# Moving eight heads' transposes from the matrix engine to the DMA crossbar, with the attention slots of a fused decoder layer planned anew

## The chip, the core and the metric

The kernel runs on one core of one Trainium2 chip. The metric is the device time of one execution in microseconds, the median of three runs; lower is better. The engines in the profile are PE (TensorE, matmuls, with PEld for its weight loads), DVE (VectorE), ACT (ScalarE), POOL (GpSimd) and SP (SyncE, which here issues DMAs only).

## What is computed

One layer of a hybrid decoder over 512 tokens of width 2048, all in float32. The normalised input is projected once and split into three attention branches; each branch's output is multiplied by SiLU of a gate path and projected back; the three are mixed by sigmoid gates, projected once more and added to the input. Cut to what matters here:

```python
proj = rms_norm(x, norm_gain) @ w_in
(qa, ka, va, za, qb, kb, vb, zb, fb, qc, zc, gate_logits) = split(proj)
# A: 12 query heads of 64, 4 key heads, sliding window of 128, blocks of 128, sinks, ALiBi
ya = sliding_window_attention(qa, ka, va, q_gain_a, k_gain_a, sinks_a)
#   p = exp(scores - m);  out = einsum('bnkgqs,bnskd->bnqkgd', p / denom, vb)
ua = (ya * silu(za)) @ w_branch_a
# B: 12 heads of 64, causal over all 512 keys, with the cumsum of log forget gates
yb = forgetting_attention(qb, kb, vb, fb + b_forget, q_gain_b, k_gain_b)
ub = (yb * silu(zb)) @ w_branch_b
# C: 4 heads of 128 into 256 memory tokens
yc = memory_attention(qc, *split(rms_norm(mem, mem_norm_gain) @ w_mem_kv), q_gain_c, k_gain_c)
uc = (yc * silu(zc)) @ w_branch_c
y = g[0] * ua + g[1] * ub + g[2] * uc          # g = sigmoid(gate_logits)
return x + y @ w_out
```

## The kernel before

**The stream.** The projections are a list of weight units. A unit is 256 rows of the weight matrix by up to 512 columns; SP loads it (`wa`), ACT rounds it to the matmul type (`wb`, two instructions, L212), DVE subtracts to get the low part (`wc`, two instructions, L215), and PE multiplies with high and low parts of the activations: high by high, low by high, high by low, 24 matmuls a unit (12 in the memory units). In the projections' order stand qB, kB, vB (branch B, two groups of six heads each: qB0, kB0, vB0, qB1, ...), qA0, qA1, kvA, z0, mem, qC, z1, z2 and z3. An unnormalised projection gathers in four PSUM banks, and an evacuation reads each bank when its last matmul is done (for V of branch B `evac` in L455 to L470, one ACT and one DVE instruction a bank).

**Slots.** Every third matmul of a unit calls `tick`, which moves the clock of slots by 0.5. Each attention head is a `Chain` of steps with an offset from the head's base slot; a step is written into the program when its slot has come and the resources that it takes (`free`: PSUM banks "T", the probability buffer "P", transposed buffers "PT", "S1", "S2", "RW" and more) are there. `later(dt, f)` writes an instruction so many slots further on. The tables at the top of the file (`BASES_*`, `STEPS_*`, `PREP_*`, `NORMS`, `EXP_*`, `DIV_*`, `LOW_*`, `PV_*`, `SUMS_X`) hold all these numbers:

```python
def tick():
    clock[0] += 0.5
    while agenda and agenda[0][0] <= clock[0]:
        heapq.heappop(agenda)[2]()
    for c in list(chains):
        c.advance()
```

PE, DVE, ACT and POOL run their instructions in the order in which they are written so. Nothing overtakes on an engine: what waits holds up all behind it.

**A head.** The keys and queries are normalised and transposed on PE (`tk`, `tq`); ACT copies the high parts and DVE subtracts the low ones (`qB`/`qA` by L547/L548, `kB`/`kA` by L558/L561, and `kl`, one of two buffers, by L559). PE makes the scores (`sB`, `sA`), twice each, with the key's high part and with `kl` (L585, L586). DVE adds the bias and takes the maximum, ACT takes the exponential with its row sums, and `scaled` (L590) divides by the sums: on DVE for branches B and C, on POOL for branch A. The probabilities `p` then have to be transposed for the product with V:

- Branch A, before: PE transposes the seven 128x128 blocks of a head (L721, L724, four and three of them, each group in a PSUM bank `ptA`), ACT casts each bank to `phA` (L565) and DVE subtracts `plA` (L567).
- Branch B, already before: POOL copies the float32 words into two planes of 16-bit halves (`s1B`), one transposing DMA turns them (`s2B`), ACT joins the halves (`ptB`, two copies, L648), ACT casts to `phB` (L656), DVE subtracts `plB` (L659).

Then PE multiplies with V (`avB`, `avA`, eight matmuls a head), ACT copies one half of the bank (`avs`) and DVE adds the other half (`ys`). When z0 is done, DVE scales its four banks (`zB`) and multiplies them into `ysB`; the sigmoid of SiLU stands on ACT much later, behind a load of its table (first at 538.7 us). `mhl` and `mraw` are the parts of the memory tokens.

After z3 the gates, the branch projections and the output projection follow, by a plan of their own.

Of the kernel before, what the change touches and what calls it, by code (L numbers as in the profile page):

```python
# [12 lines left out]
F32 = mybir.dt.float32  # L13
F32R = mybir.dt.float32r
# [22 lines left out]
BASES_C = (12.0, 19.5, 28.0, 33.5)
STEPS_B = (-11.5, -5.0, -2.5, -1.5, 0, 1, 2.0, 0.0, 3.0, 1.5, 10.0, 15.0, 17.5, 19.0, 24, 4.5)
STEPS_A = (-5.0, -1.0, -0.5, -1.5, 6.5, 8, 11, -6.5)
STEPS_C = (-8, -3.5, 0.5, 1, 8.0, 4.5, 10)  # L40

PREP_Q = ((0.0, 15.5, 41.0), (-1.5, 27.5, 50.5))
PREP_K = ((-0.5, 28.0, 40.5), (2.0, 30.5, 43.5))
PREP_A = (6, 18.5, 39.0, 46, 66.0, 76.5)
PREP_KA = (6.0, 32.5, 47.5, 68.0)

NORMS = {'qB0': (26.0, 4.5, 0.5), 'kB0': (10.5, 5.0, 3.5), 'qB1': (5.0, 3.5, 6.0), 'kB1': (6.5, 11.5, 3.5), 'qA0': (7.5, 4.0, 4.5), 'qA1': (10.0, 2.0, 1.5), 'kA': (2.5, 3, 0), 'mk': (1.0, 11.5, 6.5), 'qC0': (-1.0, 3, 0.5), 'qC1': (4.5, 7.0, 0.5)}
# [8 lines left out]
def tile_hybrid_block(ctx, tc, xT, x, memT, mem, ng, mng, w_in, b_forget, gqa, gka, sinks, gqb, gkb, gqc, gkc,  # L58
# [10 lines left out]
    def f32(ap):  # L69
        return ap.bitcast(F32)  # L70
# [521 lines left out]
    def head_B(h, kv):  # L592
# [92 lines left out]
    def head_A(h, kv):  # L685
        s = {}

        def sb():
            bi = s["bi"] = at.p.tile([P, S], F32, tag="bias", bufs=2, name=f"biA{h}")
            po.tensor_scalar(bi[:, :256], relt, -float(slopes[h]), None, op0=ALU.mult)  # L690

        def s1(pr):
            q, kh, kl, v, hv = kv()
            if pr == 0:
                p = at.p.tile([P, 1280], F32, tag="P", bufs=2, name=f"pA{h}")
                s["den"] = cp.tile([P, 16], F32, tag="den", bufs=2, name=f"denA{h}")
# [4 lines left out]
            for i in (2 * pr, 2 * pr + 1):
                c = P if i == 0 else 0
                scores(sb[:, i % 2, c:], q, kh, kl, i, slice(i * P - P + c, i * P + P))
            for i in (2 * pr, 2 * pr + 1):
                c = P if i == 0 else 0
                nm = den[:, 8 + i:9 + i]
                ve.tensor_tensor_reduce(out=pv[:, i, c:256], in0=sb[:, i % 2, c:], in1=bi[:, c:256], scale=-1.0,
                                        scalar=nsink[:, h:h + 1], op0=ALU.add, op1=ALU.min, accum_out=nm)
                later(EXP_A, lambda i=i, c=c, nm=nm: ac.activation(
                    pv[:, i, c:257], pv[:, i, c:257], AF.Exp, bias=nm, scale=-1.0, accum_out=den[:, i:i + 1]))  # L710
                later(DIV_A, lambda i=i, c=c: scaled(pv[:, i, c:256], den, i))

        def s2(g):
            pv = s["p"]
            if g == 0:
                s["hi"] = at.p.tile([P, 1280], F32R, tag="PH", bufs=1, name=f"phA{h}")
                s["lo"] = at.p.tile([P, 1280], F32R, tag="PL", bufs=1, name=f"plA{h}")
            tb = tbank(f"ptA{h}_{g}")
            c = 0
            for j in (2 * g, 2 * g + 1):  # L720
                pe.transpose(tb[:, c:c + P], pv[:, j, 128:256], ident)  # L721
# [923 lines left out]
```

## Time and profile before

| | us |
|---|---|
| median of three runs | 1470.73 (1470.09 to 1471.54) |
| the profiled execution | 1471.16 |
| its span | 1469.3 |
| PE busy | 1460.2 |
| DVE busy | 1095.3 |
| ACT busy | 759.0 |
| POOL busy | 245.6 |

The span runs from the first to the last instruction that the profiler shows; the 1.9 us between it and the execution's time lie around it. In the span, branch B's heads stand at some 110 to 355 us, branch A's at some 375 to 535, branch C's at some 540 to 615. In the rows that follow, the program's names stand without their numbers (`sB` is any head's score bank); a time in brackets is the idle time of the engine ahead of an instruction, and behind the arrow stands what ended it.

### The profile page before, as it was taken

The numbers are of one execution on the slowest core, as the hardware profiler recorded it, in microseconds if no ns is written. First come the engines' busy times: TensorE is split into PE (matmuls) and PEld (weight loads), VectorE is DVE, ScalarE is ACT, GpSimd is POOL, SyncE is SP. The second block draws the span as 40 slices with busy tenths as digits, with TensorE's granted clock in tenths as the row PEclk, the third lists the DMA queues.
The fourth block names the chain that finished last, engine by engine and source line by source line (L and its number), as shares of the span: only waits on it lengthen the run. The fifth ranks groups of instructions, "written<-read, shape, count | busy, mean of one in ns | idle before, by whom it ended". The sixth has DMA issues, their size and how long they took to land.

```text
span 1469.3 us, 20218 instructions
## 1 busy us (share of the span) xinstructions
PE 1460.2 (99%) x7073; PEld 1261.3 (86%) x7073; DVE 1095.3 (75%) x1862; ACT 759.0 (52%) x1212; POOL 245.6 (17%) x307
## 2 busy tenths in 40 slices
PE   9999999999999999999999999999999999999998
PEld 9999999988888888888888888888888888888887
DVE  6486776776687675479788788888887565689997
ACT  5546865874577564455344444444355354345442
POOL 0224762653333420000000000000000210110000
PEclk9999999999999999999999999999999999999999
DMA  8765565455355232676676676767676887666784
GB/s 294 222 205 159 132 155 161 120 143 157 108 163 158 72 101 72 206 256 221 199 236 205 221 226 214 228 209 249 208 231 214 271 237 199 222 244 220 243 293 147
DMA packets 166733, 287.35 MB, mean 196 GB/s; under 512 B 53596, under 2 KB 93148, under 8 KB 166632
## 3 DMA queue, kind: packets, MB, share of 16 engines
q1 hardware_dynamic: 161592, 269.54, 59.3%
q10 hardware_dynamic: 5040, 16.53, 3.4%
q8 instruction: 55, 0.90, 0.3%
q14 instruction: 46, 0.38, 0.1%
HBM read 244.58 MB, written 31.48 MB: 188 GB/s over the span
## 4 chain that ended last, share of the span: by engine, by line
PE 97%; ACT 2%; POOL 1%; DVE 0%; issue 0%; DMA 0%; SPq 0%; DVEq 0%; POOLq 0%; ACTq 0%
PE P L1118 41%; PE z L301 12%; PE qB L301 5%; PE vB L301 5%; PE uB L1118 4%; PE uA L1118 4%; PE kB L301 4%; PE mem L301 3%; PE qC L301 3%; PE kvA L301 3%; PE uC L1118 3%; PE qA L301 3%; PE avB L668 1%; PE avA L735 1%; ACT ptB L648 1%; PE sB L586 0%
## 5 line engine op out<-in xcount | busy, mean ns | idle before, releaser
L212 ACT CAST wb<-wa 128x512 fp32r<-128x512 f32 (+2 forms) x252 | 130.5, 567 | 150.8 <-PE z L301 33.8
L215 DVE TENSOR_TENSOR wc<-wa,wb 128x512 fp32r<-128x512 f32 (+2 forms) x252 | 151.1, 638 | 70.1 <-ACT wb L212 69.3
L1160 ACT CAST wa<-rawl 128x1024 fp32r<-128x1024 f32 x85 | 89.4, 1052 | 207.4 <-DVE rawl L1050 146.0
L1050 DVE TENSOR_TENSOR rawl<-rawl 128x512 f32<-128x512 f32 x256 | 176.9, 691 | 6.4 <-DMA rawl<-in_w_out_dram 2.0
L1434 POOL TENSOR_TENSOR y<-y,gA 128x512 f32<-128x512 f32 x16 | 28.2, 1789 | 732.2 <-DVE gA L1432 732.2
L1163 DVE TENSOR_TENSOR wc<-rawl,wa 128x1024 fp32r<-128x1024 f32 x85 | 104.9, 1234 | 51.7 <-ACT wa L1160 50.0
L1163 DVE TENSOR_TENSOR we<-rawl,wd 128x512 fp32r<-128x512 f32 (+1 forms) x128 | 122.0, 954 | 4.2 <-ACT wd L1160 0.5
L1160 ACT CAST wd<-rawl 128x512 fp32r<-128x512 f32 (+1 forms) x128 | 106.8, 834 | 24.1 <-DVE rawl L1050 21.5
L301 PE MATMUL z<-ah,wb 128*128 128x512 f32 x256 | 101.8, 398 | 0.0
L301 PE MATMUL z<-ah,wc 128*128 128x512 f32 x256 | 99.9, 390 | 0.0
L301 PE MATMUL z<-al,wb 128*128 128x512 f32 x256 | 99.8, 390 | 0.0
L1160 ACT CAST wb<-rawl 128x1024 fp32r<-128x1024 f32 x43 | 45.3, 1054 | 87.9 <-DVE rawl L1050 65.2
L1118 PE MATMUL P<-wd,xlx 128*128 128x512 f32 x192 | 74.7, 389 | 0.0
L1118 PE MATMUL P<-wd,xhx 128*128 128x512 f32 x192 | 74.7, 389 | 0.0
L1118 PE MATMUL P<-we,xhx 128*128 128x512 f32 x192 | 74.7, 389 | 0.0
L1163 DVE TENSOR_TENSOR wb<-rawl,wb 128x1024 fp32r<-128x1024 f32 x43 | 52.5, 1221 | 25.8 <-ACT wb L1160 25.6
L1047 DVE TENSOR_TENSOR R<-P,R 128x512 f32<-128x512 f32 (+1 forms) x90 | 57.0, 672 | 6.4 <-PE P L1118 5.8
L590 POOL TENSOR_SCALAR pA<-pA,denA 128x256 f32<-128x256 f32 (+1 forms) x48 | 46.0, 975 | 75.3 <-DVE denA L589 75.3
L301 PEld LDWEIGHTS z<-ah,wc 128*128 128x128 f32 x256 | 48.1, 188 | 10.2
L301 PEld LDWEIGHTS z<-ah,wb 128*128 128x128 f32 x256 | 48.1, 188 | 9.3 <-DVE zA L972 0.3
L301 PEld LDWEIGHTS z<-al,wb 128*128 128x128 f32 x256 | 48.2, 188 | 9.0
L1118 PE MATMUL P<-wa,xhx 128*128 128x512 f32 x128 | 49.8, 389 | 0.0
(411 smaller groups left out, 4248.9 us busy)
## 6 DMA issues: line engine op xcount, KB each, us to landing
rawl<-in_w_in_dram SPq DMA_DIRECT2D x144, 512.0 KB, 4.3
rawl<-in_w_out_dram SPq DMA_DIRECT2D x48, 512.0 KB, 5.0
wa<-in_w_in_dram SPq DMA_DIRECT2D x62, 384.0 KB, 3.6
wa<-in_w_in_dram SPq DMA_DIRECT2D x64, 256.0 KB, 3.0
rawl<-in_w_in_dram SPq DMA_DIRECT2D x48, 256.0 KB, 4.1
gates<-R ACTq DMA_DIRECT2D x24, 512.0 KB, 7.3
wa<-in_w_in_dram SPq DMA_DIRECT2D x16, 512.0 KB, 3.7
wa<-in_w_mem_dram SPq DMA_DIRECT2D x16, 512.0 KB, 3.6
```

The costliest lines, as they stand in the source:

```text
L212: ac.copy(hi[:, :n], raw[:, i, :n])
L215: ve.tensor_sub(lo[:, :n], raw[:, i, :n], f32(hi[:, :n]))
L301: pe.matmul(pb, a, m, start=b in fresh, stop=last and not todo[b])
L590: engine.tensor_scalar(p, p, den[:, 4 + i:5 + i], None, op0=ALU.mult)
L648: ac.copy(u16(s["t"][:, c]).rearrange("p (n e) -> p e n", e=2), s["s2"].rearrange("p (e n) -> p e n", e=2)[:, :, c])
L668: pe.matmul(av[:, j * P:], v[:, j, hv, :], t[:, BOFF[j]:BOFF[j] + n], start=(j == 0 and w == 0), stop=(j == NT - 1 and w == 1))
L1047: ve.tensor_tensor(out, a, b, op=ALU.add)
L1050: ve.tensor_tensor(out, a, b, op=ALU.subtract)
L1118: pe.matmul(*args, **kw)
L1160: ac.copy(hi[:, :k, :], src)
L1163: return lambda: ve.tensor_tensor(lo[:, :k, :], src, f32(hi[:, :k, :]), op=ALU.subtract)
L1434: po.tensor_tensor(y, y, g, op=ALU.add)
```

## The change

Eight of branch A's twelve heads (`FLIP_A`: 0, 1, 2 and 7 to 11) are transposed as branch B's are, in pieces: four POOL copies (`halves`), one transposing DMA of 128x1792 16-bit words issued by SP (`send`), two ACT copies of half the width (`join`), a cast of 896 columns on ACT (`s2h`) and a subtraction on DVE (`s2l`). Their probabilities are divided on DVE in place of POOL. Heads 3 to 6 keep the transposes on PE and the division on POOL. V of branch B lies in two tiles, four heads in one and two in the other, and so each bank is evacuated by two ACT and two DVE instructions; the second tile's place also holds the joined `ptA` later on. All tables of slots have new numbers (two lines of them are shown).

```diff
-BASES_A = (12.5, 17, 23.5, 37.5, 43, 48.5, 52, 70.5, 75.0, 79.5, 81, 89)
+BASES_A = (12.5, 17, 25.5, 37.5, 43, 48.5, 52.5, 70.5, 75.0, 78.0, 81, 89)
...
+FLIP_A = (0, 1, 2, 7, 8, 9, 10, 11)
+STEPS_F = (3.0, 4.0, 5.0, 9.5, 11.5, 12.0, 15.5)
...
-                state["v"] = tokp.tile([P, NT, nh, P], F32R, tag="V", bufs=1, name=f"V_{key}")
+                state["v"] = [tokp.tile([P, NT, 4, P], F32R, tag="V", bufs=1, name=f"V_{key}")]
+                if nh > 4:
+                    state["v"].append(tokp.tile([P, NT, 2, P], F32R, tag="V2", bufs=1, name=f"V2_{key}"))
...
-            ac.activation(v[:, b, :, 0:64], src, AF.Copy, scale=rstd[:, b:b + 1])
-            ve.scalar_tensor_tensor(out=v[:, b, :, 64:128], in0=src, scalar=rstd[:, b:b + 1],
-                                    in1=f32(v[:, b, :, 0:64]), op0=ALU.mult, op1=ALU.subtract)
+            for t, hs in zip(v, (slice(0, 4), slice(4, 6))):
+                ac.activation(t[:, b, :, 0:64], src[:, hs, :], AF.Copy, scale=rstd[:, b:b + 1])
+            for t, hs in zip(v, (slice(0, 4), slice(4, 6))):
+                ve.scalar_tensor_tensor(out=t[:, b, :, 64:128], in0=src[:, hs, :], scalar=rstd[:, b:b + 1],
+                                        in1=f32(t[:, b, :, 0:64]), op0=ALU.mult, op1=ALU.subtract)
...
-                later(DIV_A, lambda i=i, c=c: scaled(pv[:, i, c:256], den, i))
+                later(DIV_A, lambda i=i, c=c: scaled(pv[:, i, c:256], den, i, ve if h in FLIP_A else po))
...
+        def halves(i):
+            if i == 0:
+                s["s1"] = spot(0, f"s1A{h}")
+            n = P if i == 0 else 2 * P
+            o = (0, P, 3 * P, 5 * P)[i]
+            po.tensor_copy(s["s1"].rearrange("p (e n) -> p e n", e=2)[:, :, o:o + n],
+                           u16(s["p"])[:, i, 512 - 2 * n:512].rearrange("p (n e) -> p e n", e=2))
+            if i == 3:
+                release("P")
+
+        def send():
+            s["s2"] = spot(1, f"s2A{h}")
+            sy.dma_start_transpose(out=s["s2"].rearrange("p (x n) -> p x n", n=P), in_=s["s1"])
+            release("S1")
+
+        def join(n):
+            if n == 0:
+                s["t"] = tokp.tile([P, 1024], F32, tag="V2", bufs=1, name=f"ptA{h}")[:, :896]
+            c = slice(n * 448, n * 448 + 448)
+            ac.copy(u16(s["t"][:, c]).rearrange("p (n e) -> p e n", e=2),
+                    s["s2"].rearrange("p (e n) -> p e n", e=2)[:, :, c])
+            if n == 1:
+                release("S2")
+
+        def s2h():
+            s["hi"] = at.p.tile([P, 1280], F32R, tag="PH", bufs=1, name=f"phA{h}")
+            s["lo"] = at.p.tile([P, 1280], F32R, tag="PL", bufs=1, name=f"plA{h}")
+            ac.copy(s["hi"][:, :896], s["t"])
+
+        def s2l():
+            ve.tensor_tensor(s["lo"][:, :896], s["t"], f32(s["hi"][:, :896]), op=ALU.subtract)
+            release("RW")
...
+        if h in FLIP_A:
+            f = STEPS_F
+            return [(o[7], ["bias"], sb), (o[2], ["P"], lambda: s1(0)), (o[3], [], lambda: (s1(1), done())),
+                    (f[0], ["S1"], lambda: (halves(0), later(0.5, lambda: halves(1)))),
+                    (f[1], [], lambda: (halves(2), later(0.5, lambda: halves(3)))), (f[2], ["S2"], send),
+                    (f[3], ["RW"], lambda: (join(0), later(0.5, lambda: join(1)))), (f[4], ["PT"], s2h), (f[5], [], s2l),
+                    (f[6], ["T"], lambda: (s3(), release("PT")))]
```

In the order listings below, a name's numbers are those of the program: `z0_1` is bank 1 of z0, `ptB8` the transposed probabilities of B's head 8, `wb61` the high part of weight unit 61; the last number of a name only makes it unique.

PE, at the transposes of A's head 0, within z0. Before:

```order
L301 MATMUL z0_1_4145<-ah4_77,wc75_4305 128x512
L721 MATMUL ptA0_0_4422<-ident_68,pA0_4287 128x128
L724 MATMUL ptA0_0_4422<-ident_68,pA0_4287 128x128
L721 MATMUL ptA0_0_4422<-ident_68,pA0_4287 128x128
L724 MATMUL ptA0_0_4422<-ident_68,pA0_4287 128x128
L301 MATMUL z0_2_4146<-ah4_77,wb75_4304 128x512
```

After:

```order
L303 MATMUL z0_1_4156<-ah4_77,wb75_4328 128x512
L303 MATMUL z0_1_4156<-al4_85,wb75_4328 128x512
L303 MATMUL z0_1_4156<-ah4_77,wc75_4329 128x512
L303 MATMUL z0_2_4157<-ah4_77,wb75_4328 128x512
L303 MATMUL z0_2_4157<-al4_85,wb75_4328 128x512
```

The four transposes between bank 1 and bank 2 are gone, and so are the other 52 of the eight heads.

ACT, where the keys of B's heads 10 and 11 (`kB120`, `kB121`) are copied, ahead of head 10's scores, within qA1. Before:

```order
L648 COPY ptB8_3436<-s2B8_3363 128x2x640 x2
L547 ACTIVATE qB120_3458<-tqB12_3453,gs_qb_577 64x512
L547 ACTIVATE qB121_3460<-tqB12_3453,gs_qb_577 64x512
L558 ACTIVATE kB120_3467<-tkB12_3462,g_kb_606 64x512
L561 ACTIVATE kB120_3467<-tkB12_3462,g_kb_606 64x512
L558 ACTIVATE kB121_3470<-tkB12_3462,g_kb_606 64x512
L561 ACTIVATE kB121_3470<-tkB12_3462,g_kb_606 64x512
L656 CAST phB8_3487<-ptB8_3436 128x1280
L212 CAST wb61_3492<-wa61_3418 128x384 x2
```

After:

```order
L654 COPY ptB8_3415<-s2B8_3358 128x2x640
L214 CAST wb60_3438<-wa60_3387 128x384 x2
L662 CAST phB8_3455<-ptB8_3415 128x1280
L553 ACTIVATE qB120_3478<-tqB12_3473,gs_qb_577 64x512
L553 ACTIVATE qB121_3480<-tqB12_3473,gs_qb_577 64x512
L564 ACTIVATE kB120_3487<-tkB12_3482,g_kb_606 64x512
L567 ACTIVATE kB120_3487<-tkB12_3482,g_kb_606 64x512
L564 ACTIVATE kB121_3490<-tkB12_3482,g_kb_606 64x512
L567 ACTIVATE kB121_3490<-tkB12_3482,g_kb_606 64x512
L214 CAST wb61_3504<-wa61_3442 128x384 x2
```

The cast of head 8's probabilities now stands ahead of the copies. On PE, 30 rows stood between the transposes `tkB12` and the first score `sB10_0`; now 50 do, and `avB8` is among them.

DVE, where z0 ends and the memory units begin. Before:

```order
L215 TENSOR_TENSOR wc79_4581<-wa79_4528,wb79_4580 128x512
L579 TENSOR_TENSOR ysA0_4509<-avA1_4571,avsA1_4594 64x512
L972 TENSOR_TENSOR zB0_4602<-z0_1_4145,rstdb_89 128x512
L975 TENSOR_TENSOR ysB0_1701<-ysB0_1701,zB0_4602 128x1024
L567 TENSOR_TENSOR plA2_4615<-ptA2_0_4616,phA2_4614 128x512
L972 TENSOR_TENSOR zB2_4629<-z0_2_4146,rstdb_89 128x512
L972 TENSOR_TENSOR zB2_4629<-z0_3_4147,rstdb_89 128x512
L567 TENSOR_TENSOR plA2_4615<-ptA2_1_4634,phA2_4614 128x384
L975 TENSOR_TENSOR ysB1_2473<-ysB1_2473,zB2_4629 128x1024
L215 TENSOR_TENSOR wc80_4646<-wa80_4589,wb80_4645 128x512 x2
```

After:

```order
L217 TENSOR_TENSOR wc79_4581<-wa79_4509,wb79_4580 128x512
L585 TENSOR_TENSOR ysA0_4579<-avA0_4570,avsA0_4594 64x512
L770 TENSOR_TENSOR plA1_4608<-ptA1_4561,phA1_4607 128x896
L1023 TENSOR_TENSOR zB0_4604<-z0_1_4156,rstdb_89 128x512
L1026 TENSOR_TENSOR ysB0_1700<-ysB0_1700,zB0_4604 128x1024
L1023 TENSOR_TENSOR zB2_4631<-z0_2_4157,rstdb_89 128x512
L1023 TENSOR_TENSOR zB2_4631<-z0_3_4158,rstdb_89 128x512
L1026 TENSOR_TENSOR ysB1_2484<-ysB1_2484,zB2_4631 128x1024
L217 TENSOR_TENSOR wc80_4642<-wa80_4589,wb80_4641 128x512 x2
```

The two pieces of `plA2` in among the z evacuations are gone; one wide piece, `plA1`, stands ahead of them all.

More of the change, by code (lines that the diff above doesn't have):

```diff
@@ L33 @@
 BOFF = (0, 512, 1024, 896)
-BASES_B = ((8, 20, 32.0, 39.5, 51, 63.5), (8.0, 19.5, 34.5, 42.0, 55.5, 67.0))
-BASES_A = (12.5, 17, 23.5, 37.5, 43, 48.5, 52, 70.5, 75.0, 79.5, 81, 89)
[L37 to L47, printed above, removed]
+BASES_B = ((7.0, 20.5, 32.0, 39.5, 49.5, 62.0), (6.5, 19.5, 31.5, 39.5, 58.0, 64.5))
+BASES_A = (12.5, 17, 25.5, 37.5, 43, 48.5, 52.5, 70.5, 75.0, 78.0, 81, 89)
+BASES_C = (12.5, 20.0, 26.5, 30.5)
+STEPS_B = (-11.5, -5.0, -3.5, -1.5, 0, 1, 2.0, 1.0, 3.0, 1.5, 11.5, 15.0, 18.0, 19.0, 24, 4.5)
+STEPS_A = (-5.0, 3.5, -0.5, -2.5, 6.5, 8, 11, -7.0)
+FLIP_A = (0, 1, 2, 7, 8, 9, 10, 11)
+STEPS_F = (3.0, 4.0, 5.0, 9.5, 11.5, 12.0, 15.5)
+STEPS_C = (-8, -4.5, 0.5, 0, 8.0, 6.0, 12.5)
+PREP_Q = ((-5.5, 15.5, 41.0), (-6.0, 27.5, 51.0))
+PREP_K = ((-2.0, 29.5, 39.0), (1.0, 25.0, 37.5))
+PREP_A = (9.5, 15.5, 39.5, 46, 66.0, 74.5)
+PREP_KA = (6.0, 33.0, 47.0, 67.0)
+NORMS = {'qB0': (25.5, 4.0, -0.5), 'kB0': (8.5, 10.5, -2.0), 'qB1': (5.0, 2.5, 6.0), 'kB1': (6.5, 13.5, 3.5), 'qA0': (9.0, 14.0, 8.5), 'qA1': (24.0, 9.0, -2.0), 'kA': (7.0, 5.5, -2), 'mk': (1.0, 17.0, 2.0), 'qC0': (-1.5, 4.0, 0.5), 'qC1': (6.5, 9.5, 2.0)}
 LOW_W, LOW_M, LOW_Q, LOW_K, LOW_P = ((1.0, 1), (0.5, 1.5), 0.5, 1.0, 0.5)
-EXP_B, EXP_A, EXP_C, DIV_B, DIV_A, DIV_C = (2.5, 0.5, 1.0, 3.5, 3.5, 3.0)
+EXP_B, EXP_A, EXP_C, DIV_B, DIV_A, DIV_C = (2.5, 1.5, 1.0, 3.5, 2.0, 3.0)
 PV_B, PV_A = ((2.0, 2.0), (0.5, 1))
-SUMS_X = (6, 13, 19.0, 132.5, 109.5, 208.5, 194.0, 235.5)
+SUMS_X = (1.0, 13.0, 19.0, 132.5, 109.5, 213.5, 202.5, 231.0)
 @with_exitstack
@@ L667, in s3 @@
                 for w, t in enumerate((s["hi"], s["lo"])):
-                    pe.matmul(av[:, j * P:], v[:, j, hv, :], t[:, BOFF[j]:BOFF[j] + n],
+                    pe.matmul(av[:, j * P:], v[hv // 4][:, j, hv % 4, :], t[:, BOFF[j]:BOFF[j] + n],
                               start=(j == 0 and w == 0), stop=(j == NT - 1 and w == 1))
@@ L727, in s2, with spot @@
             split(s["hi"][:, o:o + c], s["lo"][:, o:o + c], tb[:, :c])
+        def spot(n, name):
+            if h < 6:
+                return spare(n, name, U16, 1792)
+            return u16(place(6 + n, name)).rearrange("p i n -> p (i n)")[:, :1792]
+        def halves(i):
[26 more added lines that the diff above has]
+            release("RW")
         def s3():
@@ L734, in s3 @@
                 for w, t in enumerate((s["hi"], s["lo"])):
-                    pe.matmul(av[:, j * P:j * P + n], v[:, j, hv, :], t[:, j * 256:j * 256 + n],
+                    pe.matmul(av[:, j * P:j * P + n], v[0][:, j, hv, :], t[:, j * 256:j * 256 + n],
                               start=(j == 0 and w == 0), stop=(j == 3 and w == 1))
```

## Prediction

> **What bounds the kernel now.** I read the page's busy times first, then the chain of work that ended last, then the waits of TensorE.
>
> ```profile
> PE 1460.2 (99%) x7073; PEld 1261.3 (86%) x7073; DVE 1095.3 (75%) x1862; ACT 759.0 (52%) x1212; POOL 245.6 (17%) x307
> ...
> PE 97%; ACT 2%; POOL 1%; DVE 0%; issue 0%; DMA 0%; SPq 0%; DVEq 0%; POOLq 0%; ACTq 0%
> ```
>
> TensorE is busy for 1460.2 us and is 97% of the chain. So three things move the time: matmuls taken from TensorE, its waits, and the rate at which it runs. Work on the other engines costs only where TensorE comes to wait for it. These are its waits inside the part that is replanned (us in total, times, longest us):
>
> ```profile
> PE sB L586 <- DVE kl L559: 1.3, 1, 1.3
> PE kB L301 <- DVE wc L215: 0.8, 2, 0.6
> ...
> PE kB L301 <- ACT wb L212: 0.2, 1, 0.2
> ```
>
> They come to 2.3 us, but their rows in TensorE's timeline (start, duration) say that the first costs more than its 1.3 us:
>
> ```profile
> 296.75 0.22 PE L585 MATMUL sB<-kB,qB 128*128 128x128 f32 x1
> 298.23 0.33 PE L586 MATMUL sB<-kl,qB 128*128 128x128 f32 x1 [1.26 <-DVE kl L559]
> ...
> 300.48 0.41 PE L585 MATMUL sB<-kB,qB 128*128 128x256 f32 x1
> 300.70 0.41 PE L586 MATMUL sB<-kl,qB 128*128 128x256 f32 x1
> 300.91 0.52 PE L301 MATMUL qA<-wb,ah 128*128 128x384 f32 x1
> ...
> 303.15 0.39 PE L301 MATMUL qA<-wc,ah 128*128 128x384 f32 x1
> 303.38 0.34 PE L301 MATMUL qA<-wb,al 128*128 128x384 f32 x1
> 303.55 0.33 PE L301 MATMUL qA<-wb,ah 128*128 128x384 f32 x1
> ```
>
> ```profile
> 300.00:301.00 1.00, 1.00 (x5) 1.00 (x5) 0.97 (x4) 0.75 (x2) 0.09 (x1) 0.50 0.00 0
> ```
>
> From 300.91 to 303.15 seven matmuls start, one each 0.32 us; at full rate the step is 0.17 us (303.38 to 303.55). The column after the five engines is the granted clock: 0.50. Between 296.75 and 303.38 stand 14 matmuls of 384 columns (2.4 us at 0.17) and four short score matmuls (300.48 to 300.70 is 0.22 us at the halved clock, so about 0.11 each at full rate, 0.45 together): 2.9 us in place of 6.63, so this stall costs 3.7 us, of which about 2 are the halved clock. Its cause stands on ScalarE and VectorE:
>
> ```profile
> 293.20 1.38 ACT L547 ACTIVATE qB<-tqB,gs_qb 64x512 fp32r<-64x512 f32 x2
> 294.60 0.69 ACT L558 ACTIVATE kB<-tkB,g_kb 64x512 fp32r<-64x512 f32 x1
> ...
> 296.71 0.69 ACT L561 ACTIVATE kB<-tkB,g_kb 64x512 fp32r<-64x512 f32 x1
> 297.43 1.53 DVE L559 SCALAR_TENSOR_TENSOR kl<-tkB,g_kb,kB 64x512 fp32r<-64x512 f32 x2 [1.28 <-ACT kB L561]
> ```
>
> kl starts when the fourth copy ends (297.40). The other two waits are one place, around kB1:
>
> ```profile
> 169.01 0.34 PE L301 MATMUL kB<-wb,ah 128*128 128x384 f32 x1
> 169.99 0.44 PE L301 MATMUL kB<-wc,ah 128*128 128x384 f32 x1 [0.64 <-DVE wc L215]
> ...
> 174.44 0.44 PE L301 MATMUL kB<-wb,ah 128*128 128x384 f32 x1 [0.18 <-ACT wb L212]
> 175.03 0.45 PE L301 MATMUL kB<-wc,ah 128*128 128x384 f32 x1 [0.15 <-DVE wc L215]
> ```
>
> The step to 169.99 is 0.98 us, 0.81 over 0.17; that to 175.03 is 0.59, 0.42 over; at 174.44 about 0.35 and behind the three some 0.2 are lost. In sum 1.8 us.
>
> **Term 1, the transposes.** Eight heads lose seven transposes each: 56 of 7073 matmuls. What a group of four costs:
>
> ```profile
> 389.54 0.40 PE L301 MATMUL z<-ah,wc 128*128 128x512 f32 x1
> 389.77 0.27 PE L721 MATMUL ptA<-ident,pA 128*128 128x128 f32 x1
> ...
> 390.13 0.48 PE L301 MATMUL z<-ah,wb 128*128 128x512 f32 x1
> 390.44 0.39 PE L301 MATMUL z<-al,wb 128*128 128x512 f32 x1
> ```
>
> Without transposes 389.54 to 390.44 would be two steps of 0.23 (389.54 to 389.77 is one): 0.90 − 0.46 = 0.44 us a group, 0.11 a transpose. 56 × 0.11 = 6.2; a group of three pays its end, too, so I take 0.80 a head: **−6.4 us**.
>
> **What takes their place.** Per flipped head (min/median/max ns):
>
> ```profile
> L633 POOL COPY s1B<-pB x72: 393/510/1769, 123.1 to 335.6; 128x384 uint16<-128x384 uint16 x48, 128x256 uint16<-128x256 uint16 x12, 128x512 uint16<-128x512 uint16 x12
> DMA to landing us min/median/max: 4.1/4.2/5.4
> L648 ACT COPY ptB<-s2B x24: 1635/1651/1672, 133.5 to 342.6; 128x1280 uint16<-128x1280 uint16 x24
> L656 ACT CAST phB<-ptB x12: 1252/1258/1279, 138.7 to 345.2; 128x1280 fp32r<-128x1280 f32 x12
> L659 DVE TENSOR_TENSOR plB<-ptB,phB x12: 1473/1485/1811, 140.4 to 347.2; 128x1280 fp32r<-128x1280 f32 x12
> L590 POOL TENSOR_SCALAR pA<-pA,denA x48: 605/926/1933, 383.2 to 522.7; 128x256 f32<-128x256 f32 x36, 128x128 f32<-128x128 f32 x12
> L590 DVE TENSOR_SCALAR pC<-pC,denC x16: 352/353/355, 552.3 to 602.5; 128x256 f32<-128x256 f32 x16
> L565 ACT CAST phA<-ptA x24: 464/535/589, 390.7 to 530.3; 128x512 fp32r<-128x512 f32 x12, 128x384 fp32r<-128x384 f32 x12
> L567 DVE TENSOR_TENSOR plA<-ptA,phA x24: 543/615/694, 392.3 to 531.3; 128x512 fp32r<-128x512 f32 x12, 128x384 fp32r<-128x384 f32 x12
> ```
>
> The second row is the transposing DMA of branch B. ScalarE: two joins of 896 elements (1.65 × 896/1280 = 1.16 each) and one cast of 896 (0.90), less two casts (1.07): +2.2 us a head, 17 in all. VectorE: one subtraction of 896 (1.07) for two (1.23), and four scalings taken from POOL (up to 0.35 each, 1.3): +1.1 a head, 9 in all. POOL: less 4 × 0.93, plus four copies of about 0.5–0.6: lighter. SP gets eight more DMAs; send stands 4.5 slots ahead of join, a slot being six matmuls of 0.23, 6.2 us against a landing of 4.2, with 5.4 at the worst. Is there room? Branch A's stretches (PE, PEld, DVE, ACT, POOL busy):
>
> ```profile
> 380.00:420.00 40.00, 40.00 (x210) 33.62 (x209) 29.74 (x76) 21.06 (x50) 14.17 (x15) 1.00 0.37 117
> 420.00:460.00 40.00, 40.00 (x216) 33.77 (x216) 34.39 (x99) 32.90 (x80) 19.32 (x18) 1.00 0.58 184
> 460.00:500.00 40.00, 40.00 (x211) 33.70 (x210) 27.76 (x71) 25.60 (x58) 12.96 (x14) 1.00 0.36 105
> ```
>
> The twelve heads follow each other at some 13 us, three to a row. Heads 3 to 6, which stay as they were, lie in the second row, where ScalarE has 7 us left. In the first and third, 3 × 2.2 = 6.6 us more makes 28 and 32 of 40, and VectorE 33 and 31. So I cost this at nothing; the cover is that slack, and where a join or cast stands ahead of a weight cast at the wrong moment it is gone (term 4). V of branch B in two tiles makes two instructions of one on both engines in eight evacuations, at the same number of elements. What an instruction more costs I take from the casts: 512 and 384 elements apart are 1.07, 896 in one would be 0.90, so some 0.2 us on ScalarE and as much on VectorE, before banks that are free for most of a unit: 0 (0 to 0.3).
>
> [...]
>
> **Term 2, the stall at 296.75.** In the new order 50 rows stand between the transposes of B10's keys and its first score, where 30 did: 42 of 384 columns (7.3 us at 0.173) and the eight of avB8, 2560 columns in all (1.15), so 8.4 us of TensorE for 5.2. Ahead of the first kl's end now stand phB8's cast, the query copies, four key copies and the kl itself: 1.26 + 1.38 + 2.76 + 0.77 = 6.2 of these 8.4. The wait and the halved clock go, −3.7. But the low part of weight unit 61 still stands behind the second kl on VectorE (0.77 and some 0.5 of its own, 7.4 in all, or 6.2 if phB8's cast is done before the transposes) and is needed after 31 matmuls and avB8, 6.5 us. Left: about 0.5. **−3.2 us** (−3.7 to 0, the end where a new wait again halves the clock).
>
> **Term 3, the stall at 169.** The transposes of B2's keys stand eight matmuls earlier against wc35, avB1's, 1.15 us as above; wc35's 0.8 goes, the second half (ptB2's pieces ahead of wb36) keeps its order: **−1.2 us** (−1.8 to −0.4).
>
> **Term 4, new waits.** All slots are moved, so I went through the queues at the first need of each product. Four places have no room left by these durations. (a) Branch A's first scores: 15 matmuls of 0.23 (3.5 us) between its keys' transposes and the first score, 36 before; the copies and kl need 4 × 0.69 + 0.77 = 3.5 and the hops between: +0.3 (0 to 0.5). (b) The start of the mem units:
>
> ```profile
> L972 DVE TENSOR_TENSOR zB<-z,rstdb x6: 679/686/692, 408.2 to 579.0; 128x512 f32<-128x512 f32 x6
> L975 DVE TENSOR_TENSOR ysB<-ysB,zB x3: 1216/1225/1226, 411.0 to 579.7; 128x1024 f32<-128x1024 f32 x3
> ```
>
> Behind plA1 VectorE does one zB, ysB0, two zB, ysB1 and the first piece of wc80 (the size of a zB): 0.69 + 1.22 + 1.37 + 1.22 + 0.69 = 5.2 us. TensorE has 25 matmuls of 0.23 and four transposes of 0.11 from the end of z0's bank 1 to the first use of wc80, 6.2. So wc80 is late if plA1 ends more than 1 us behind that bank; it waits for phA1, which stands behind two mhl0 pieces and avsA0 on ScalarE and comes with 0.90 of its own. I put that at 0.5 us late, and wc81, behind kl1, at as much: +1.0 (0 to 1.5). (c) z1's last bank, which is qC's: its copies stand behind joins on ScalarE: +0.25 (0 to 0.5). (d) avA11, whose cast now stands behind z's table load and two sigmoids on ScalarE: +0.35 (0 to 1). Each is of the kind of the waits at kB1 (0.2 to 0.6), which left the clock alone. **+1.9 us** (0 to 3.5).
>
> **The sum**, against the profiled execution's 1471.16 us (span 1469.3 and 1.9 around it): −6.4 − 3.2 − 1.2 + 1.9 = −8.9, so 1462.3. That execution is 0.4 above the median of 1470.73, so 1461.8 as a median. From the transposes on, the projections, branches and outputs keep their order on TensorE.
>
> **Rivals.** (1) New waits as dear as the old: terms 2 to 4 cancel, and only the transposes count: 1470.7 − 6.4 = 1464.3. For it: the same planner rules and a queue as tight; against it, the counted 50 rows. (2) One of the waits of term 4 grows over about 1.3 us and halves the clock, 3.7 us in place of 0.3 to 1: about 1465, two of them 1468. The row for it is the 0.50 after 1.26 us of idling; against it, the 0.64 at kB1 that did not. [...] (3) Slower: ScalarE becomes the bound in the flipped heads. Its joins queue behind weight casts, each head's phA comes late, and weight casts behind the joins come late as well, with a stall of 3.7 us each. It decides from three stalls on (11.1 against the 10.8 gained by terms 1 to 3): 1471 to 1475. Against it: 28 and 32 us of 40. (4) No new wait at all: −6.4 − 3.7 − 1.8 = −11.9, about 1458.8.
>
> **Chances.** Forecast (1460 to 1463.5) 0.42, (1) 0.18, (2) 0.20, (3) 0.06, (4) 0.14. The range 1458.4 to 1467.6 takes in (4), (1) and most of (2). 0.2%, 2.9 us, is about what a measurement of this kernel can tell from no change: faster is below 1467.8. That is the forecast, (1), (4) and most of (2), 0.87; the rest of (2) and a mild (3) 0.08; slower 0.05, nearly all of (3).
>
> **What would show it.** Right: TensorE's matmuls 56 fewer and its busy time about 9 us less; no row with a granted clock of 0.50 between 290 and 310; wc61 waited for by half a microsecond; small waits on wc80 and wc81 and at avA11; ScalarE near 28 and 32 us in the first and third stretch. Wrong: a granted clock near 0.50 anywhere in 380 to 540, ptA or phA as what TensorE waits for several times, or the stall at sB back in its full length.

## The result, and the profile after

The changed kernel takes 1462.73 us (median of six runs, 1462.48 to 1463.62); the kernel before took 1470.91 beside it (six runs, 1470.07 to 1472.03). The ratio is 0.9946, with a 95% interval of 0.9933 to 0.9958: 8.2 us faster, where 1461.8 (9.1 less than the 1470.91) was forecast. One run of a kernel further down (the doubled transposes: 1620.72 us, at a mean granted clock of 0.851 where its other runs have 0.999 to 1.000) is left out of that kernel's median. The profiled execution took 1462.48 us, 8.7 less than the profiled one before; the sum that the forecast was made from said 8.9.

The page of the changed kernel, busy times and chain (lines that answer to those at the start of the prediction):

```profile
PE 1452.0 (99%) x7017; PEld 1254.0 (86%) x7017; DVE 1111.1 (76%) x1894; ACT 776.3 (53%) x1228; POOL 230.9 (16%) x307
...
PE 96%; ACT 2%; DVE 1%; DMA 0%; issue 0%; DVEq 0%; ACTq 0%
```

The matmuls are 56 fewer, TensorE's busy time is 8.2 us less, and it is the bound as before. ScalarE has 17.3 us more (17 forecast), VectorE 15.8 (9 forecast): the divisions taken from POOL are 12.8 of it in place of some 10, and the low parts `wc`, which are the same instructions as before, take 3.4 more in sum (154.5 for 151.1). TensorE's waits (us in total, times, longest us):

```profile
PE mem L303 <- DVE wc L217: 1.4, 2, 0.9
PE avA L779 <- DVE plA L770: 0.4, 1, 0.4
PE kB L303 <- DVE wc L217: 0.2, 1, 0.2
```

The waits for kl and the first one at kB1 are gone; two at the memory units and one at avA11 are new. Their rows in TensorE's timeline, and the place of the old stall in the table of stretches (the granted clock is the third column from the end):

```profile
412.03 0.50 PE L303 MATMUL mem<-wc,mhl 128*128 128x512 f32 x1 [0.51 <-DVE wc L217]
...
423.79 0.50 PE L303 MATMUL mem<-wc,mhl 128*128 128x512 f32 x1 [0.88 <-DVE wc L217]
...
533.84 0.38 PE L779 MATMUL avA<-plA,V_vA 128*128 128x256 f32 x1 [0.44 <-DVE plA L770]
```

```profile
300.00:301.00 1.00, 1.00 (x8) 1.00 (x7) 0.93 (x5) 1.00 (x2) 0.24 (x1) 1.00 0.23 72
```

What the flipped heads cost on the other engines, by tile (min/median/max ns), and the landing of their transposing DMAs:

```profile
L759 ACT COPY ptA<-s2A x16: 1202/1210/1226, 387.1 to 525.7; 128x896 uint16<-128x896 uint16 x16
L767 ACT CAST phA<-ptA x8: 926/938/946, 389.4 to 531.7; 128x896 fp32r<-128x896 f32 x8
L770 DVE TENSOR_TENSOR plA<-ptA,phA x8: 1074/1092/1093, 390.4 to 532.7; 128x896 fp32r<-128x896 f32 x8
L596 DVE TENSOR_SCALAR pA<-pA,denA x32: 286/355/790, 377.1 to 510.3; 128x256 f32<-128x256 f32 x24, 128x128 f32<-128x128 f32 x8
DMA to landing us min/median/max: 3.4/3.4/5.2
```

They are within 5% of the prices that were scaled from branch B's (1.16, 0.90, 1.07, 0.35 us), and the DMA, of 896 columns where B's has 1280, lands in 3.4 us and not 4.2. The stretches of branch A (PE, PEld, DVE, ACT, POOL busy):

```profile
380.00:420.00 40.00, 39.49 (x198) 33.12 (x197) 33.33 (x81) 29.23 (x60) 8.57 (x13) 1.00 0.55 148
420.00:460.00 40.00, 39.03 (x215) 32.77 (x214) 34.12 (x87) 31.86 (x74) 18.52 (x19) 1.00 0.53 172
460.00:500.00 40.00, 40.00 (x202) 33.87 (x202) 33.91 (x101) 28.04 (x64) 11.21 (x15) 1.00 0.41 115
```

ScalarE stands at 29 and 28 us in the first and third (28 and 32 forecast); the cover held there.

### The profile page after: what moved, and what is told of

Same layout as the page of the kernel before. It is cut to its first block, busy times and chain, and to the rows that moved or that the text cites. A ratio compares the mean times of both kernels' runs of the same rounds, so it can differ in the third digit from the quotient of the medians.

```text
span 1460.7 us, 20197 instructions
## 1 busy us (share of the span) xinstructions
PE 1452.0 (99%) x7017; PEld 1254.0 (86%) x7017; DVE 1111.1 (76%) x1894; ACT 776.3 (53%) x1228; POOL 230.9 (16%) x307
## 4 chain that ended last, share of the span: by engine, by line
PE 96%; ACT 2%; DVE 1%; DMA 0%; issue 0%; DVEq 0%; ACTq 0%
PE P L1169 42%; PE z L303 11%; PE qB L303 5%; PE qA L303 5%; PE vB L303 5%; PE uB L1169 4%; PE uA L1169 4%; PE kB L303 4%; PE qC L303 3%; PE kvA L303 3%; PE uC L1169 3%; PE mem L303 2%; PE avB L674 1%; PE avA L779 1%; PE sB L592 1%; PE sB L591 0%
## 5 line engine op out<-in xcount | busy, mean ns | idle before, releaser
L217 DVE TENSOR_TENSOR wc<-wa,wb 128x512 fp32r<-128x512 f32 (+2 forms) x252 | 154.5, 652 | 81.7 <-ACT wb L214 73.2
L1169 PE MATMUL P<-wa,xlx 128*128 128x512 f32 x128 | 49.8, 389 | 0.0
```

The costliest lines, as they stand in the source:

```text
L217: ve.tensor_sub(lo[:, :n], raw[:, i, :n], f32(hi[:, :n]))
L1169: pe.matmul(*args, **kw)
```

## The experiments

Ratios are against the kernel before, run on the same chip: its median is 1471.41 us beside the first four kernels below, 1470.91 beside the next three and 1471.42 beside the version with nine flipped heads. Differences to the changed kernel's 1462.73 us are taken across chips, and so they are good to about the 0.5 us by which the kernel before differs.

**Each transpose twice (the kernel before).**

```diff
-                pe.transpose(tb[:, c:c + P], pv[:, j, 128:256], ident)
+                for _ in range(2):
+                    pe.transpose(tb[:, c:c + P], pv[:, j, 128:256], ident)
```

and the same for the second kind.

> The kernel before, with each of branch A's 84 transposes done twice into the same place; nothing else differs. My account (a transpose is a matmul on the bound engine, 0.11 us each, hidden behind nothing): 84 x 0.11 = +9.2 us, about 1480 us. Rival: most of the 0.44 us of a group of four is the switch into and out of the transposes, and the next matmul's weight load hides the rest; then 24 groups stay 24 groups, and the time grows by under 4 us.

1479.73 us (three runs), ratio 1.0057 (1.0040 to 1.0074): 8.3 us for 84 transposes, 0.099 each (0.07 to 0.13 by the interval). In TensorE's timeline they start 0.109 us apart. The rival's 4 us lie outside the interval: the price is per transpose, not per group, and nothing hides it here. By their spacing 56 of them are 6.1 us.

**Branch B's slots alone, and all but them.** In the kernel before, the lines `BASES_B`, `STEPS_B`, `PREP_Q`, `PREP_K` and B's entries of `NORMS` are the changed kernel's; in the other kernel it is the reverse.

```diff
-BASES_B = ((8, 20, 32.0, 39.5, 51, 63.5), (8.0, 19.5, 34.5, 42.0, 55.5, 67.0))
+BASES_B = ((7.0, 20.5, 32.0, 39.5, 49.5, 62.0), (6.5, 19.5, 31.5, 39.5, 58.0, 64.5))
...
-PREP_K = ((-0.5, 28.0, 40.5), (2.0, 30.5, 43.5))
+PREP_K = ((-2.0, 29.5, 39.0), (1.0, 25.0, 37.5))
```

> The kernel before, with only branch B's slot tables (bases, steps, preparation of queries and keys, norms) taken from the changed kernel; branch A as before, no flips. My account: the stalls at 297 and at 169 to 175 us go as they did in the changed kernel, 3.8 + 1.1 = -4.9 us, about 1466.0. Rival: these stalls go only because the flips change what stands beside them, or they come up elsewhere in branch B; then 1470.9 as before.

1467.24 us, ratio 0.9971 (0.9960 to 0.9981): −4.2.

> The changed kernel, with branch B's slot tables put back to those of before. My account (the parts add up): the two stalls come back, 1462.7 + 4.9 = 1467.6. Rival (the parts are one plan, and B's old slots collide with A's new ones): over 1470.

1466.18 us, ratio 0.9966 (0.9955 to 0.9978): 3.45 more than the changed kernel, with the old stall back at its old place (TensorE's waits):

```profile
PE sB L592 <- DVE kl L565: 1.1, 1, 1.1
```

So the slots of branch B are worth 3 to 4 us by themselves, with or without the flips: the parts add up within the intervals, which are some 1.7 us to either side, and the rivals of both runs fall. Both values are below the 4.9 us that the profiled executions give. A likely reason is in the last experiment: in 20 of 46 further executions of the kernel before the stall did not halve the clock.

**No flips, in the new slots.**

```diff
-FLIP_A = (0, 1, 2, 7, 8, 9, 10, 11)
+FLIP_A = ()
```

> The changed kernel with no head flipped: all twelve heads transposed on TensorE and divided on POOL, in the new slots. My account: 56 transposes come back at 0.11 each, +6.2 us, and the new waits at the memory units and at avA11 (2.4 us) go, since plA1's place, the joins and the table load no longer stand in their way: 1462.7 + 6.2 - 2.4 = 1466.5. Rival: the new waits belong to the new slots and not to the flips: 1468.9 or more.

1468.64 us, ratio 0.9981 (0.9972 to 0.9991), 5.9 more than the changed kernel. I had expected all the new waits to go with the flips; one did not:

```profile
PE mem L303 <- DVE wc L217: 0.6, 1, 0.6
```

One wait at the memory units stays (at 426.35, where the changed kernel has 0.88 at 423.79): it belongs to the new slots. The one at unit 81 and the one at avA11 are gone: they belong to the flips. So 5.9 us is a net gain. From the first projection to the last microseconds the changed kernel waits for 2.0 us by these lists, this one for 1.2, and the price of the 56 transposes alone lies that much above the difference: some 6.7 us by the medians, 6.2 by the profiled spans (1466.1 and 1460.7 us), beside the 6.1 by their spacing.

**Division back on POOL.**

```diff
-                later(DIV_A, lambda i=i, c=c: scaled(pv[:, i, c:256], den, i, ve if h in FLIP_A else po))
+                later(DIV_A, lambda i=i, c=c: scaled(pv[:, i, c:256], den, i, po))
```

> The changed kernel, with the flipped heads' division by the sums back on POOL (0.93 us each for 0.35 on VectorE). POOL is then busy for 9 of 40 us more in the flipped stretches, well under full, but the copies into halves stand behind the divisions on it: four divisions of 0.93 end about 1.2 us later than four of 0.35 that wait for their exponentials, and the send has 6.2 us of slots for a landing of 4.2. My account: just covered, and VectorE is relieved by 9 us: 1462 to 1463.5. Rival: the halves come late, the transposing DMA lands late, and avA waits: 1465 or more.

1467.71 us, ratio 0.9978 (0.9968 to 0.9987), 5.0 more than the changed kernel: the rival, and the waits were not where even that had put them. Waits of TensorE, then ScalarE's timeline at two joins that stand without their data, and around the worst wait:

```profile
PE mem L303 <- DVE wc L217: 2.0, 3, 0.9
...
PE z L303 <- ACT t_qC L448: 1.5, 1, 1.5
PE mem L303 <- DVE zB L1023: 1.1, 1, 1.1
```

```profile
399.00 2.29 ACT L759 COPY ptA<-s2A 128x896 uint16<-128x896 uint16 x2 [1.27 <-DMA s2A<-s1A]
...
514.38 2.29 ACT L759 COPY ptA<-s2A 128x896 uint16<-128x896 uint16 x2 [1.00 <-DMA s2A<-s1A]
...
522.09 2.28 ACT L759 COPY ptA<-s2A 128x896 uint16<-128x896 uint16 x2
524.20 0.88 ACT L448 ACTIVATE t_qC<-qC,rstds 128x256 f32<-128x256 f32 x2
```

POOL's timeline shows what the copies into halves now stand behind:

```profile
506.58 3.70 POOL L596 TENSOR_SCALAR pA<-pA,denA 128x128 f32<-128x128 f32 x4
510.23 0.61 POOL L745 COPY s1A<-pA 128x512 uint16<-128x512 uint16 x1
```

The last copy of one head stands behind the four divisions of the next, which take the 4 × 0.93 us of the median. Its transposing DMA is issued when that copy is done, at 510.87; it lands late, and ScalarE waits a microsecond for it with everything that stands behind the join. The next join, both pieces in a row, pushes the evacuation of qC's last bank, and z1 waits 1.5 us for that bank. The same happened at 399.00: phA1 behind that join starts at 403.47, in the changed kernel at 400.37, and the `zB` that the first memory unit waits for is late with it. The first of these DMAs is issued 3.0 us later than in the changed kernel (383.6 for 380.6), where I had worked out 1.2. I had booked the division's move as 1.3 us a head of VectorE's time, at no value; it keeps the send on time.

**All twelve heads flipped.**

```diff
-FLIP_A = (0, 1, 2, 7, 8, 9, 10, 11)
+FLIP_A = tuple(range(12))
```

> The changed kernel with all twelve heads flipped, the other slots unchanged. The transposes of heads 3 to 6 go, -3.2 us. ScalarE gets 4 x 2.2 = 8.8 us more in the stretch 416 to 456, where it is busy for 32.6 of 40, VectorE 4 x 1.1 beside 35.7. My account: both are then full there, weight casts come late, and two to four waits of 1 to 3.7 us take the gain: 1463 to 1470. Rival: the queues still find room, since the unit's slack takes the backlog: 1459.5.

1475.02 us, ratio 1.0028 (1.0017 to 1.0039): slower than the kernel before, and by more than my range. Waits of TensorE:

```profile
PE qC L303 <- DVE V_C L1000: 5.4, 1, 5.4
PE mem L303 <- DVE wc L217: 4.2, 6, 1.8
```

The second line is the one I had expected, six late weights. The first is something else; POOL, SP's queue and ScalarE show it:

```profile
462.58 2.11 POOL L745 COPY s1A<-pA 128x256 uint16<-128x256 uint16 x4 [15.12 <-PE mem L303]
```

```profile
462.79 4.93 SPq L204 DMA_DIRECT2D wa<-in_w_in_dram  x2
468.87 1.97 SPq L752 DMA_TRANSPOSE s2A<-s1A  x1
```

```profile
473.97 1.18 ACT L759 COPY ptA<-s2A 128x896 uint16<-128x896 uint16 x1 [4.53 <-DMA s2A<-s1A]
475.03 0.67 ACT L999 ACTIVATE V_C<-mem,rstds 128x512 fp32r<-128x512 f32 x1
```

Head 6's copies into halves stood behind the end of the memory units, since their place in memory is free only then; its transposing DMA then followed weight loads on SP; the join stood in ScalarE's queue without its data for 4.5 us; V_C, behind it, released qC's next matmul. This is the mechanism of rival 3 in kind, a join ahead of what TensorE needs, but by lateness of the DMA and not by a full ScalarE (33.9 of 40 us from 416 to 456). VectorE had 37.9 of these 40 us, nearly all, and the late weights are its low parts. The clock halved as well: it was 0.50 for 3.4 us behind the longest of the six waits (1.77 us, to 448.06) and for 6.8 us from inside the wait for V_C on, and every run of this kernel has a mean clock of 0.997 or 0.998.

**Two tries at a better version.** The first moves three slots, the second flips head 6 as well and puts the additions and sigmoids later:

```diff
-PREP_KA = (6.0, 33.0, 47.0, 67.0)
+PREP_KA = (6.0, 34.0, 47.0, 67.0)
...
-PREP_A = (9.5, 15.5, 39.5, 46, 66.0, 74.5)
+PREP_A = (9.5, 15.5, 40.5, 46, 66.0, 74.5)
```

with the base of head 11 at 89.5.

> The changed kernel with three slots moved against the three new waits: the preparation of A's second key head from 33 to 34 (kl1 then stands behind the low part of unit 81), that of its third query pair from 39.5 to 40.5 (its copies behind unit 84's cast), and the base of head 11 from 89 to 89.5. My account: the waits of 0.51, 0.88 and 0.44 us with the loss behind them (2.3 us in all) go: 1460.5. Rival: each comes up one instruction on: 1462.7.

1464.08 us, ratio 0.9951 (0.9935 to 0.9968): no gain, 1.3 us over the changed kernel. TensorE's waits:

```profile
PE mem L303 <- DVE wc L217: 1.2, 2, 0.7
PE tkA L546 <- DVE plA L573: 0.6, 1, 0.6
```

```diff
-FLIP_A = (0, 1, 2, 7, 8, 9, 10, 11)
+FLIP_A = (0, 1, 2, 6, 7, 8, 9, 10, 11)
...
-            if h < 6:
+            if h < 7:
...
-            pv_out(av, ysv("A", h // 2)[(h % 2) * 64:(h % 2) * 64 + 64, :], h % 2, f"avsA{h}", PV_A)
+            pv_out(av, ysv("A", h // 2)[(h % 2) * 64:(h % 2) * 64 + 64, :], h % 2, f"avsA{h}", PV_A if h != 1 else (0.5, 2))
...
-                dt = (70, 73, 74) if c == 0 else (8, 13, 19) if c == 3 else (1, 4, 5)
+                dt = (70, 73, 74) if c == 0 else (8, 13, 19) if c == 3 else (3.5, 5.5, 6.5)
```

> The changed kernel with three edits: head 6 flipped, too (its copies in the place that heads 0 to 5 use); head 1's addition into ysA one slot later, so that the first low part of unit 81 stands ahead of it; the sigmoids of z1 and what follows them 1.5 to 2.5 slots later, so that phA11 stands ahead of the table load. My account: seven transposes go (-0.8), the wait of 0.51 at unit 81 goes (-0.7), that of 0.44 at avA11 goes (-0.6): 1460.6. Rival (as in the version with three moved slots, each wait comes up one instruction on, and head 6's late send adds one): 1463 to 1465.

1467.44 us, ratio 0.9972 (0.9960 to 0.9983), worse than the changed kernel by 4.7. TensorE waits for V_C, behind head 6's joins, and elsewhere:

```profile
PE qC L303 <- DVE V_C L1000: 0.9, 1, 0.9
```

Both times most of the waits came up again, some instructions further on, and the one at avA11 stayed (0.43 and 0.45 us). No version that beats the changed kernel was found.

**The clock.** Four runs, of one execution each, ask when a wait halves it. The two ladders make the low part of five weight units late (`LATE` lists the units and the extra subtractions, here those of the first ladder):

```diff
+    LATE = {114: 9, 116: 10, 118: 11, 123: 6, 125: 12}
...
+        extra = LATE.get(nsplit[0], 0)
...
-                ve.tensor_sub(lo[:, :n], raw[:, i, :n], f32(hi[:, :n]))
+                for _ in range(1 + (extra if i == 0 else 0)):
+                    ve.tensor_sub(lo[:, :n], raw[:, i, :n], f32(hi[:, :n]))
```

> The changed kernel, with the low part of five weight units in z2 and z3 made late: the first of its two subtractions is done 10, 11, 12, 7 and 13 times over (the same values again, 0.62 us each). From the slack of 4.5 us that these units have, TensorE should wait about 1.0, 1.6, 2.2, 0.6 and 2.9 us. My account (an idle stretch over some 1.2 us halves the granted clock for about 4 us, which costs 2 to 2.5 us beside the wait): the waits of 0.6 and 1.0 cost themselves, the other three show a granted clock near 0.50 and cost 2 us more each, in all 8.3 + 6 to 7.5, about 1478. [...]

The waits were 1.0, 2.5, 3.3 and 6.3 us (one unit was not late), the time 1484.54 us, 6.5 over my account: the waits come to 13.0 us where I had 8.3, since a subtraction took 0.71 us there and not 0.62. Behind the 2.5:

```profile
607.68 0.50 PE L309 MATMUL z<-ah,wc 128*128 128x512 f32 x1 [2.48 <-DVE wc L223]
```

```profile
608.00:609.00 1.00, 1.00 (x6) 0.78 (x5) 1.00 (x3) 0.00 (x0) 0.00 (x0) 1.00 0.00 0
609.00:610.00 1.00, 1.00 (x4) 0.81 (x3) 1.00 (x3) 0.00 (x0) 0.00 (x0) 0.59 0.55 98
610.00:612.00 2.00, 2.00 (x6) 1.59 (x5) 0.63 (x2) 0.00 (x0) 0.00 (x0) 0.50 0.85 236
612.00:613.00 1.00, 1.00 (x4) 0.77 (x4) 0.00 (x0) 0.00 (x0) 0.00 (x0) 0.70 0.88 269
```

TensorE is back at work at 607.68, and the clock halves only 1.5 us later. At 0.59 a fraction of 0.82 of its microsecond is at half clock, at 0.70 one of 0.60: 0.82 + 2 + 0.60 = 3.4 us. The wait of 3.3 us was followed by 0.50 for 3.4 us, too; in that of 6.3 us the clock halved while TensorE still waited, for 6.8 us; that of 1.0 left it alone.

> As the first ladder, with 11, 8, 8, 7 and 5 extra subtractions (each was 0.71 us there) on the same five units. By the first ladder's rows TensorE should wait about 1.3, 1.1, 1.3, 1.7 and 1.3 us. So far a wait of 1.0 never halved the clock and one of 1.8 or more always did, while the same 1.25 us wait for kl did in two kernels and did not in a third. [...] Rival (a fixed length decides, 1.2 us or so): all of 1.3 and more show 0.50, that of 1.1 not, and 1476. Rival (what decides is what else ran, and VectorE's long subtractions never did it at this length): none, 1469.5.

Waits of 1.48, 0.99, 1.13 and 1.70 us, and 1469.94 us; the clock stayed at 1.00 behind every one, the longest at 648.96:

```profile
648.96 0.50 PE L309 MATMUL z<-ah,wc 128*128 128x512 f32 x1 [1.70 <-DVE wc L223]
```

```profile
648.00:652.00 4.00, 3.04 (x13) 2.50 (x14) 3.97 (x7) 2.09 (x3) 0.00 (x0) 1.00 0.96 351
```

I had counted on half clock behind at least one, which did not come, and the rival that a fixed 1.2 us decides is refuted. The other rival, that what else ran decides, forecast 1469.5 and fits this run; nothing here refutes it. Last, the kernel before, unchanged:

> The kernel before, unchanged, profiled once more. The wait for kl at 297 us should be there again with 1.2 to 1.3 us. [...] Rival (the place decides): 0.50 at 300 to 303 us each time.

> As the run above, a third execution of the same program: 0.50 or 1.00 at 300 to 303 us by chance by my account, 0.50 by the rival.

The waits for kl were 1.26 and 1.25 us; the clock in the two runs, and in the kernel with double transposes, where the same wait was 1.25:

```profile
299.00:300.00 1.00, 0.85 (x2) 0.59 (x3) 1.00 (x3) 1.00 (x3) 0.00 (x0) 0.81 0.00 0
300.00:303.00 3.00, 3.00 (x12) 3.00 (x12) 2.30 (x5) 1.46 (x3) 2.28 (x1) 0.50 0.58 167
```

```profile
300.00:301.00 1.00, 1.00 (x6) 1.00 (x7) 0.97 (x4) 1.00 (x3) 0.00 (x0) 0.87 0.00 0
301.00:304.00 3.00, 3.00 (x11) 3.00 (x10) 2.07 (x5) 1.46 (x1) 2.84 (x2) 0.50 0.60 175
```

```profile
300.00:303.00 3.00, 3.00 (x18) 2.94 (x18) 2.50 (x6) 1.46 (x3) 2.07 (x1) 1.00 0.56 152
```

The half clock begins at about 299.6 in the one execution, at 300.7 in the other, and not at all in the third kernel, with the same instructions around. The rival of these two runs came true in both, but that kernel, which is the same program up to this place, speaks against it: neither the place nor the length of this wait decides alone. What differs between these executions is set out in the last section, as far as the traces show it. How often it happens: of the 46 further runs of the kernel before that are listed with their mean granted clock, 15 have 0.998 (mean 1471.70 us), 11 have 0.999 (1471.40), 20 have 1.000 (1470.82). A stretch of 3.4 us at half clock takes 0.0012 off the mean, so the 20 had none; another half-clock stretch begins in the last microseconds of the span (in the changed kernel at 1459.5 of 1460.7), so that 0.999 can be the one or the other. With branch B's slots alone, all eight have 1.000.

## Why the prediction was right, point by point

**Term 1, the transposes (−6.4).** Right within the measurement: 56 × 0.109 = 6.1 us by their spacing, 5.5 by the doubled ones (3.9 to 7.3 by the interval), 6.2 to 6.7 between the kernels with and without flips when the difference in waits is taken out. The 0.02 us a head that I added for a group's end is not seen.

**What takes their place (nothing).** Right, but with less room than I said. The prices and ScalarE's busy time came as worked out; VectorE's grew by 15.8 us for 9, without a wait that I can put down to that. That the same cover is gone four heads further (1475.02 us) and one division later (1467.71) shows that it rests on the DMA's being on time, as the queues of POOL and SP decide it, more than on ScalarE's and VectorE's busy shares, from which I argued.

**Term 2, the stall at 296.75 (−3.2).** In the profiled executions it is −3.8 (by the steps between TensorE's starts, against its usual 0.173): the whole stall is gone. The 0.5 us that I kept for unit 61's low part did not come. That step was wrong because I weighed phB8's cast as half in the way; the keys are transposed from 290.15 on, and the cast, started at 289.10, is over by 290.4:

```profile
289.10 1.26 ACT L662 CAST phB<-ptB 128x1280 fp32r<-128x1280 f32 x1
```

In the median, on the other hand, the stall was worth less than 3.7: I took the clock of one profiled execution for that of all, and 20 of 46 runs of the kernel before show none of it. Branch B's slots alone gave 4.2 us, of which term 3 is 1.1, so some 3.1 are left for this stall. Two errors of opposite sign, and that their sum came so close to the 3.2 is luck.

**Term 3, the stall at 169 (−1.2).** Right: −1.1, wc35's wait gone and wc36's left, as the 0.2 us in the list of waits shows.

**Term 4, new waits (+1.9).** Somewhat low: the spans differ by 8.6, terms 1 to 3 are −11.0, and +2.4 is left for new waits; the list has 1.4 and 0.4, the rest is lost right behind them. Right in kind for two of four places. (a) and (c) did not come (0.55 together). (b) was mis-sized, about 1.7 at two units for 1.0 (their steps are 0.67 and 1.04 over the usual): unit 81 was late as forecast, but unit 84 was late in place of unit 80. VectorE's timeline shows why: unit 81's low part stands behind kl1, a piece of mhl1 and ysA, unit 84's behind the low parts of the next queries, which wait for ScalarE.

```profile
409.27 0.75 DVE L565 SCALAR_TENSOR_TENSOR kl<-tkA,g_ka,kA 64x512 fp32r<-64x512 f32 x1
410.05 0.48 DVE L980 SCALAR_TENSOR_TENSOR mhl<-mraw,mngt,mhl 128x256 fp32r<-128x256 f32 x1
410.57 0.69 DVE L585 TENSOR_TENSOR ysA<-avA,avsA 64x512 f32<-64x512 f32 x1
411.28 1.29 DVE L217 TENSOR_TENSOR wc<-wa,wb 128x512 fp32r<-128x512 f32 x2
...
421.49 1.52 DVE L554 SCALAR_TENSOR_TENSOR qA<-tqA,gs_qa,qA 64x512 fp32r<-64x512 f32 x2 [0.66 <-ACT qA L553]
423.04 1.49 DVE L217 TENSOR_TENSOR wc<-wa,wb 128x512 fp32r<-128x512 f32 x2
```

(d) came as said, 0.44 of waiting, about 0.6 with what follows it. ScalarE's rows:

```profile
527.60 1.28 ACT L1034 ACT_TABLE_LOAD   x1
528.89 2.00 ACT L1034 ACTIVATE zB<-zB 128x1024 f32<-128x1024 f32 x2
...
531.73 0.93 ACT L767 CAST phA<-ptA 128x896 fp32r<-128x896 f32 x1
```

**The rivals.** (1) fell with the kl wait, though its point about new waits was half right: without flips, the new slots keep one of them. (2) had a wait of 0.88 us as its longest, below the 1.3 us of its condition, and the clock stayed at 1.00. (3) did not happen here, and does with four heads more.

## What to carry to other kernels

On TensorE, the bound engine here, a transpose that was taken away was worth its spacing in that engine's timeline (0.109 us, not its duration of 0.27), and it counted as long as what replaced it was on time; what had to be on time was the whole way through the queues: the versions whose transposing DMA came late (joins waited 1.0 and 1.3 us for it with POOL's divisions, 4.5 with twelve heads) lost 5.0 and, beside other waits, 12.3 us to the one where it came in time. A wait that the profile of one execution shows with a halved clock should be priced with and without it, since other executions of the same program may not have it (20 of 46 here did not). Moving single slots of such a plan against single waits gave nothing: most waits came up again a few instructions further on.

## What the runs showed of the hardware

TensorE's clock after a wait, in the profiled executions: each stretch at 0.50 that followed a wait of up to 3.3 us lasted 3.4 us (behind the 2.5 us wait above, and 0.26 + 3 + 0.16 with the third execution of the kernel before, whose next microsecond was at 0.92), and it began up to 2.3 us after TensorE was back at work, at a time that differs between executions of one program (1.6, 1.6 and 2.3 us behind the stall at kl in the three profiles of the kernel before). Behind waits of 5.4 and 6.3 us it lasted 6.8 us, twice as long, and began before they ended.

Two executions show such stretches behind more than one wait, by the granted clock of the microseconds at their ends. In the first ladder the clock is at 0.50 from 609.19 to 612.60, from 626.25 to 629.66 and from 670.63 to 677.45 us; with twelve heads it falls to it at 448.42 and at 475.72. The starts lie 5 and 13 times 3.41 us apart in the ladder and 8 times with twelve heads, and the lengths are one or two times the same 3.41. In the executions with the stall at kl the start is at 299.83 (the first profile of the kernel before), 299.6, 300.7 and, with branch B's slots put back, 300.5.

TensorE's idle time in the 3.41 us ahead of the start was 1.43 us in the first profile of the kernel before (296.42 to 299.83: the whole wait of 1.26 and the short gaps behind it), and 1.43, 1.31 and 1.29 us in the three others. With double transposes the wait was 1.25 us, the steps behind it were the same (0.35 and 0.59 us between TensorE's starts, where 0.17 is usual), and the clock stayed at 1.00. So a wait of 1.12 to 1.26 us with such steps behind it was followed by half clock in four of the five profiled executions with the stall at kl, while waits of 1.48 and 1.70 us in the second ladder and of 1.54 with POOL's divisions were not. The other half-clock stretches that followed waits of up to 3.3 us had 1.77 (twelve heads), 1.91 and 2.35 us (first ladder) of idle time in the 3.41 us ahead of them. What decides was not settled.

By its length a stretch of 3.4 us at half clock costs 1.7 us. Whole runs leave the cost between 0.9 us (the 46 runs of the kernel before, 0.998 against 1.000) and 2.1 (with B's slots put back, the runs with a mean clock of 0.998 took 1467.75 and 1468.18 us, those with 1.000 took 1465.33 to 1466.31).
